# Feed-forward column pairs as seven block products of input sums, and a window V load divided at row 2

## The chip, the cores and the metric

The kernel runs on one core of one Trainium2 chip. The metric is the device time of one execution in microseconds. The kernel before took 1517.5 us in the median of three runs (1512.81 to 1521.79).

## What is computed

One step of a decoder layer for 520 tokens: a prompt of 512 and 8 sampled tokens. The core of the reference, cut:

```python
x = x + 0.5 * swiglu(rms_norm(x, ffn1_norm), ffn1_w_in, ffn1_w_out)
mixed, state = token_mixers(rms_norm(x, mix_norm), ...)
x = x + mixed
x = x + 0.5 * swiglu(rms_norm(x, ffn2_norm), ffn2_w_in, ffn2_w_out)
return rms_norm(x, final_norm), state

def swiglu(h, w_in, w_out):          # w_in 1024 x 5632, w_out 2816 x 1024
    a, b = split(h @ w_in, 2)
    return (silu(a) * b) @ w_out
```

The mixers are a causal convolution group and an attention group with three branches (compressed, selected and sliding-window keys and values); the sampled tokens read paged caches and a window of 512 earlier tokens of each sequence. Everything is float32.

## The kernel before

**Layout.** Activations lie transposed: 128 partitions hold features, 520 columns hold tokens, so X is 8 tiles (k = 0 to 7) of 128 x 520. `HALF` names the two token halves of 260 columns. A product in float32 is made of three matmuls in a reduced format (`mm3`): weight high x input high, weight high x input low, weight low x input high, where high is a rounded copy (made on ACT by `acp`) and low is the rest (made on DVE or POOL by a subtraction).

**Stages.** The program runs in this order: compression of the cached keys and values (`compress`), the first feed-forward layer, the input projection, convolution and attention under a planner (`Threads`, which keeps a modelled clock for each engine and always steps the earliest thread), the output projection (`t_wout`), the second feed-forward layer, the final norm (`tail`). In the feed-forward layers nothing is planned: the order is the order of the code.

**A feed-forward layer** (`ffn`, line 763) works in three groups of 8, 7 and 7 column pairs (`GROUPS`). A column pair is 128 gate columns and 128 value columns of `w_in`. For each pair and each token half it makes the gate product and the value product over k = 0 to 7, each in a PSUM bank of its own: 2 x 2 x 8 x 3 = 96 matmuls of 128x260. Then `gate` (silu on ACT), `value` (the product with the gate on DVE, its high part on ACT) and `low` (its low part on DVE) follow, one step later each. In the second layer the norm is not in the inputs: `gate` and `value` first multiply the PSUM result by `r`. After a group come four output blocks (`d2`) of `w_out` columns with four accumulations each, added to X on DVE.

**Weights** (`Units`, line 711). A block of weights is 1 MB, loaded on SP's queue into one of two buffers `wraw` (tag raw). It is cut into units of 128x512: for each unit ACT makes the high part and DVE the low part in one of 4 tiles `wb` of two units each, so at most 8 units are ahead of TensorE. `step` issues the pending low parts, at most one new unit, the matmuls, and then what the plan holds for this step. When the last low part of a block has been issued, `w_dma` issues the load of the block after the next.

**Around the layers.** The first layer's inputs `xh`, `xl` are normalised while `compress` runs (`xp_scale`, `xp_low`). `bg` holds small work on the compressed keys (`kc_root`, `kc_norm`) of which one piece goes behind each block of the first layer; `bg_out` holds transposes (`kc_trans`, `conv_state`) for the last group's output blocks. The compressed V, `vcs`, stays in buffer B1 from the compression until attention reads it.

**The window** (`win_load`, line 1682). For a sampled sequence b, the window buffer holds 512 positions as 128 rows of 4 x 128 values; one position, the first quarter of row 0, is that of the new token and comes from `ksm`. Keys are loaded as 128 rows and V as three DMAs: rows 1 to 127 (line 1688), the rest of row 0 (line 1689), the new token (line 1690). Two sequences' keys go to a buffer of their own and the others, with all V, rotate through four buffers `kwr`, so that V of sequences 4 to 7 is loaded when TensorE has read V of sequences 0 to 3. All of them are issued on SP's queue, in order.

Names in the profile: pb is a PSUM bank; xh and xl the layer's inputs; wb the weight units; gh and gl the gated products; late the window buffers; sg the gathered selected blocks; misc holds ksm; line 120 is the helper that issues every engine instruction.

Of the kernel before, what the change touches and what calls it, by code (L numbers as in the profile page):

```python
# [19 lines left out]
NB = 8  # L20
# [13 lines left out]
PF = 2  # L34
XP = 0
# [171 lines left out]
def tile_step(ctx: ExitStack, tc: tile.TileContext, I, O, off):  # L207
# [318 lines left out]
    vcs = new("B1", [2, NB, 128], F32, "vcs")  # L526
    hl_i = [0]
# [12 lines left out]
    def compress():  # L540
# [69 lines left out]
        soft.append(lambda: cmp_second(*pend, 5))  # L610
# [7 lines left out]
    def xp_scale(k):  # L618

        if k == 0:  # L620
            X1["h"] = rows("A2", 8, F32R, "xh")
            X1["l"] = Rows([new("B0", [4, T], F32R, "xl"), None])
        if k == 4:
            X1["l"].tiles[1] = new("A1", [4, T], F32R, "xl")
        t = X1["t"] = tmp([T])
        tt(t, X[:, k], R["r0"], ALU.mult)
        acp(X1["h"][:, k], t, scale=g1(k))
# [4 lines left out]
    def u_start():  # L632
        U1.append(Units(0))
# [77 lines left out]
    class Units:  # L711


        def __init__(self, c0):
            self.c, self.list, self.pp, self.hl, self.low = c0, [], 0, {}, []
            self.pf, self.n = PF if c0 else 8, {}
            for j0, n in GROUPS:
                for j in range(n + 4):
                    self.n[c0] = 2048 if j < n else n * 256
                    self.list += [(c0, q) for q in range(4)]  # L720
                    c0 += 1
            self.left = [2] * (len(self.list) // 2)

        def more(self):
# [4 lines left out]
            c, q = self.list[i_]  # L729
            if i_ % 2 == 0:  # L730
                self.cur = new(("WH", "WL")[i_ // 2 % 2], [2, 2, 512], F32R, "wb", 2)
            m = min(512, self.n[c] - q * 512)
            x = wraw[c][:, q * 512:q * 512 + m]
            h, l = self.cur[:, i_ % 2, 0, :m], self.cur[:, i_ % 2, 1, :m]
# [6 lines left out]
            if q == 3:  # L741
                self.low.append(c)
            self.pp += 1
            return True

# [13 lines left out]
        def used(self, c):  # L759
            for q in range(4):  # L760
                self.left[self.hl.pop((c, q))[2]] -= 1

    def ffn(U, xh, xl, normed, bg, next_prep, g_tiles, tail=None, out=(), last=None):
# [3 lines left out]
        r = None if normed else new("r", [T])  # L767
# [4 lines left out]
        def step(work):  # L772
            nonlocal q_
            U.lows()
            U.more()
# [7 lines left out]
        if r is not None:  # L783
            put(0, lambda: norm_root(r, R["acc"], D, (6, 7)), partial(recip, 0), partial(recip, 1))
            put(1, partial(recip, 2), partial(recip, 3))
        while soft:
            put(0, soft.pop(0))
        for gi, (j0, n) in enumerate(GROUPS):
            gh, gl = g_tiles(n)
            for j in range(n):  # L790
                for h in range(2):
                    o_ = (2 * j + h + (0 if n == 8 else 2)) % 4 * 2
                    pa, pb = [ps.tile([128, 512], F32, name="pb", tag="b%d" % (o_ + s_))[:, :TH] for s_ in range(2)]
                    t = tmp([2, TH])

                    def prods(o, s_, h=h):
                        first = gi == 0 and j == 0
                        for k in range(8):
                            w_ = U.parts(c, k, s_ * 128)
                            mm(o, w_[0], xh[:, k, HALF[h]], k == 0, False)  # L800
                            if not first:
                                mm(o, w_[0], xl[:, k, HALF[h]], False, False)
                            mm(o, w_[1], xh[:, k, HALF[h]], False, k == 7 and not first)
                        for k in range(8) if first else ():
                            mm(o, U.parts(c, k, s_ * 128)[0], xl[:, k, HALF[h]], False, k == 7)

                    def gate(t=t, pa=pa, h=h):
                        if r is not None:
                            tt(t[:, 0], pa, r[:, HALF[h]], ALU.mult)
                            pa = t[:, 0]  # L810
                        ACT.activation(t[:, 0], pa, AF.Silu)

                    def value(t=t, pb=pb, h=h, g=gh[:, j, HALF[h]]):
                        if r is not None:
                            tt(t[:, 1], pb, r[:, HALF[h]], ALU.mult)
# [1372 lines left out]
```

## Time and profile before

| | before |
|---|---|
| median of 3 runs, us | 1517.5 (1512.81 to 1521.79) |
| the profiled execution, us | 1514.12 |
| its span, first to last instruction, us | 1512.3 |
| mean granted TensorE clock | 0.957 |
| TensorE busy | 1378.9 us, 91% |
| DVE busy | 835.3 us, 55% |
| ACT busy | 597.8 us, 40% |
| POOL busy | 321.8 us, 21% |
| HBM traffic | 108 GB/s over the span |

The profile is one execution. A line of its groups names the source line, engine, operation, output <- inputs, shape and count, then busy time and the mean length of one in ns, then the engine's idle time just before and what ended it. Matmuls overlap, so the length of one (283 ns) is not what one costs; cost is taken from counts per time. A busy share is an average over stages with different limits, so each stage is read by itself.

### The profile page before, as it was taken

Reading aid. Unit: us, or ns where it says so; the run is one execution under the profiler, and the core shown is the slowest. Engines: PE = TensorE matmul, PEld = TensorE weight load, DVE = VectorE, ACT = ScalarE, POOL = GpSimd, SP = SyncE. Lnnn points to the kernel's source line nnn. Section 1 sums busy time; section 2 is a strip of 40 time slices with the busy share of each in tenths; the row PEclk is TensorE's granted clock in tenths of the full one; section 3 lists DMA queues with packets and bytes.
Section 4 is the critical chain, followed back from the end, with each engine's and each line's share of the span. In section 5 each row is a group of like instructions: output and inputs, shape, how many; then the busy total and the mean of one; then the engine's idle time right before and its main releaser. Section 6 shows DMA issues by size and latency. Waiting matters only on the chain.

```text
span 1512.3 us, 25566 instructions
## 1 busy us (share of the span) xinstructions
PE 1378.9 (91%) x10375; PEld 1271.8 (84%) x10375; DVE 835.3 (55%) x1670; ACT 597.8 (40%) x1280; POOL 321.8 (21%) x286
## 2 busy tenths in 40 slices
PE   3999898999999999997888899926899999999997
PEld 2778676999999999997686776716899999999997
DVE  3777789334334433679796556624684534444444
ACT  2445455333232233456566635404343322322333
POOL 4556755000000000145464022113220000000000
PEclk8999999999999999999899889958799999999999
DMA  5846353222332333242129035405133233233321
GB/s 170 250 144 195 112 163 116 57 85 84 110 87 74 109 86 111 83 141 79 36 86 222 28 83 161 147 29 136 61 96 96 84 101 96 81 99 87 95 102 57
DMA packets 168824, 160.25 MB, mean 106 GB/s; under 512 B 9013, under 2 KB 150933, under 8 KB 168507
## 3 DMA queue, kind: packets, MB, share of 16 engines
q1 hardware_dynamic: 153859, 109.33, 24.3%
q0 software_dynamic: 14848, 49.29, 10.9%
q8 instruction: 81, 1.33, 0.4%
q14 instruction: 36, 0.29, 0.1%
HBM read 152.65 MB, written 10.60 MB: 108 GB/s over the span
## 4 chain that ended last, share of the span: by engine, by line
PE 39%; DVE 7%; ACT 3%; SPq 3%; DMA 2%; issue 1%; POOL 0%; DVEq 0%; POOLq 0%; ACTq 0%
PE pb L120 39%; SPq L1689 2%; DVE cv L120 1%; DVE tmp L120 1%; DVE wl L120 1%; DVE misc L120 1%; ACT pz L120 1%; DMA late<-misc 1%; ACT tmp L120 0%; ACT L120 0%; ACT wh L120 0%; DMA sg<-in_cache_v_sel,idxs 0%; DVE su L120 0%; SPq L322 0%; DVE usm_v L120 0%
## 5 line engine op out<-in xcount | busy, mean ns | idle before, releaser
L120 PE MATMUL pb<-xh,wb 128*128 128x260 f32 x2816 | 501.5, 283 | 0.8 <-ACT wb L120 0.5
L120 PEld LDWEIGHTS pb<-xh,wb 128*128 128x128 f32 x2816 | 430.2, 188 | 1.4 <-ACT wb L120 0.7
L120 PE MATMUL pb<-xl,wb 128*128 128x260 f32 x1408 | 387.9, 282 | 0.0
L120 PEld LDWEIGHTS pb<-xl,wb 128*128 128x128 f32 x1408 | 261.0, 188 | 0.0
L120 PE MATMUL pb<-gh,wb 128*128 128x260 f32 x1408 | 256.6, 283 | 0.0
L120 ACT ACTIVATE wb<-wraw 128x512 fp32r<-128x512 f32 (+1 forms) x272 | 161.1, 610 | 175.7 <-PE pb L120 158.8
L120 PEld LDWEIGHTS pb<-gh,wb 128*128 128x128 f32 x1408 | 218.0, 188 | 0.0
L120 PE MATMUL pb<-gl,wb 128*128 128x260 f32 x704 | 198.7, 282 | 0.0
L120 DVE TENSOR_TENSOR wb<-wraw,wb 128x512 fp32r<-128x512 f32 (+1 forms) x262 | 174.7, 667 | 2.1
L120 PEld LDWEIGHTS pb<-gl,wb 128*128 128x128 f32 x704 | 132.5, 188 | 0.0
L120 PE MATMUL pb<-hl,w1hl 128*128 128x512 f32 x384 | 99.3, 408 | 14.2 <-DVE hl L120 13.8
L120 DVE TENSOR_TENSOR tmp<-pb,r 128x260 f32<-128x260 f32 x104 | 43.6, 426 | 123.2 <-PE pb L120 123.2
L120 DVE TENSOR_TENSOR hl<-tmp,hl 128x512 fp32r<-128x512 f32 x128 | 92.7, 724 | 32.1 <-ACT hl L120 18.5
L120 DVE SCALAR_TENSOR_TENSOR X<-pb,X 128x260 f32<-128x260 f32 x96 | 41.0, 428 | 123.8 <-PE pb L120 123.8
L120 DVE TENSOR_TENSOR tmp<-pb,tmp 128x260 f32<-128x260 f32 x44 | 18.9, 429 | 161.8 <-PE pb L120 157.1
L120 ACT ACTIVATE gh<-tmp 128x260 fp32r<-128x260 f32 x88 | 37.2, 423 | 171.9 <-DVE tmp L120 170.2
L120 ACT ACTIVATE hl<-tmp 128x512 fp32r<-128x512 f32 x128 | 79.1, 630 | 62.0 <-DVE tmp L120 50.3
L120 PEld LDWEIGHTS pb<-hl,w1hl 128*128 128x128 f32 x384 | 70.5, 190 | 38.5 <-DVE hl L120 23.3
L120 DVE STREAM_TRANSPOSE tmp<-craw 128x512 f32<-128x512 f32 x128 | 89.6, 701 | 23.5 <-issue 10.3
L120 PE MATMUL pb<-hl,w1h 128*128 128x512 f32 x256 | 85.6, 412 | 4.8 <-DVE hl L120 2.9
L120 POOL TENSOR_TENSOR wl<-wraw,wh 128x512 fp32r<-128x512 f32 (+1 forms) x23 | 34.9, 1519 | 215.8 <-ACT wh L120 204.8
L120 POOL DMA_INDIRECT craw<-in_cache_k_cmp,idxc x64 | 63.9, 998 | 57.8 <-DVE tmp L120 33.3
(307 smaller groups left out, 2319.5 us busy)
## 6 DMA issues: line engine op xcount, KB each, us to landing
wraw<-in_ffn_w_in SPq DMA_DIRECT2D x88, 512.0 KB
wraw<-in_ffn_w_out SPq DMA_DIRECT2D x16, 896.0 KB
wraw<-in_ffn_w_out SPq DMA_DIRECT2D x8, 1024.0 KB
wraw<-in_w_in SPq DMA_DIRECT2D x8, 512.0 KB
wraw<-in_w_in SPq DMA_DIRECT2D x4, 1024.0 KB
wraw<-in_w_out SPq DMA_DIRECT2D x4, 1024.0 KB
xs<-X SPq DMA_DIRECT2D x1, 2080.0 KB
X<-xs SPq DMA_DIRECT2D x8, 260.0 KB
```

What stands on the lines that cost most here:

```text
L120: r = fn(*a, **k)
L1689: SP.dma_start(t_[0:1, 128:512], src[0:1, 128:512])
```

## The change

It has two parts, and the buffers and order that they need.

**Seven products.** Each layer gets a string of kinds per group, one letter for each pair: P plain, S seven products. The change is announced as 16 of 22 pairs; `KINDS1` and `KINDS2` hold 14 letters S each. For an S pair the inputs are four blocks (two token halves by two halves of k) and the weights four blocks (two halves of k by gate and value). Seven products of 4 k-tiles each, of blocks or of sums of blocks (Winograd's form), replace eight. Four of the weight operands are differences made on DVE in the raw buffer or in a temporary; the four input sums (`Sums`) are made once per layer, from normalised inputs, on POOL, with their high and low parts on ACT and DVE. The results are put together by additions on DVE as they leave PSUM. Two of the banks are read by DVE after their first product and written again by TensorE later. In the second layer the blocks themselves are also normalised once (`blocks`, `b21`), so pairs after the first four need no multiplication by `r`.

**Pace and order.** P pairs now go through all four banks for every quarter of k, so that a unit is used up in one step of 24 matmuls (12 in an S step). `pace` issues units at a rate that depends on the kind (0.9 a step in S, 1.5 in P, 1.25 in output blocks), `need` makes one that isn't there. The first output block of each group goes by quarters of k too.

**Buffers.** B1, D0, D1, D2 and A1 hold the sums. So the compressed V is written to DRAM after the compression (`vsp`) and read back in the last group's output blocks; `kc_trans` and `conv_state` come 6 places later there.

**The window.** V is loaded as rows 2 to 127, then columns 128 to 511 of rows 0 and 1, then the first quarter of row 1, then the new token.

The core of the diff:

```diff
+KINDS1 = "PPPSSPSS", "SSPSSPS", "SSPSSPS"
+KINDS2 = "PPPPSSSS", "SSPSSPS", "SSPSSPS"
+RATE = {"S": .9, "P": 1.5, "O": 1.25}
...
+        def last():
+            cmp_second(*pend, 5)
+            SP.dma_start(vsp, vcs)
+        soft.append(last)
...
+        def source(self, c, q):
+            if self.kind[c] != "S":
+                m = min(512, self.n[c] - q * 512)
+                return wraw[c][:, q * 512:q * 512 + m]
+            v = wraw[c][:, :2048].rearrange("p (k h e) -> p k h e", k=8, h=2)
+            b11, b12, b21, b22 = v[:, 0:4, 0], v[:, 0:4, 1], v[:, 4:8, 0], v[:, 4:8, 1]
+            if q == 1:
+                tt(b11, b12, b11, ALU.subtract)
+                self.t2 = tmp([4, 128])
+                tt(self.t2, b22, b11, ALU.subtract)
+            if q == 2:
+                tt(b12, b22, b12, ALU.subtract)
+            if q == 5:
+                tt(b21, b21, self.t2, ALU.subtract)
+            return (b11, self.t2 if q else None, b12, b11, b21, b21, b22)[q]
...
+        def pace(self, rate):
+            self.credit = min(self.credit + rate, 2.5)
+            self.lows()
+            while self.credit >= 1 and self.more():
+                self.credit -= 1
+                if self.credit >= 1:
+                    self.lows()
...
+                for o_, p_, q_, op in ((st[0][:, 0], a[:, HALF[1]], b[:, HALF[1]], ALU.add),
+                                       (st[0][:, 1], None, a[:, HALF[0]], ALU.subtract),
+                                       (st[1][:, 0], a[:, HALF[0]], a[:, HALF[1]], ALU.subtract),
+                                       (st[1][:, 1], b[:, HALF[0]], None, ALU.subtract)):
+                    POOL.tensor_tensor(o_, st[0][:, 0] if p_ is None else p_, st[0][:, 1] if q_ is None else q_, op=op)
...
-        def step(work):
+        def step(work, kind):
             nonlocal q_
-            U.lows()
-            U.more()
+            U.pace(RATE[kind])
             work()
...
+        for kk in range(4):
+            for i_ in range(3):
+                put((1 if normed else 3) + 3 * kk + i_ - (kk > 2 and normed),
+                    lambda kk=kk, i_=i_: parts_.setdefault(kk, SX.prep(kk, r, gname))[i_]())
...
+        def seven(c, j, bk, G):
+            p_, q2, r_, s_ = bk
...
+            s0 = q_
+            put(s0 + 1, lambda: acp(u[:, 0], p_))
+            put(s0 + 2, lambda: tt(u[:, 0], q2, u[:, 0], ALU.add))
+            put(s0 + 3, lambda: tt(u[:, 1], r_, u[:, 0], ALU.add))
+            put(s0 + 4, lambda: tt(tb[:, 1], s_, u[:, 1], ALU.add))
+            put(s0 + 5, lambda: ACT.activation(ta[:, 0], p_, AF.Silu))
+            put(s0 + 6, lambda: tt(tb[:, 0], r_, u[:, 0], ALU.add),
+                lambda: ACT.activation(tb[:, 0], tb[:, 0], AF.Silu))
+            put(s0 + 7, lambda: tt(ta[:, 1], s_, u[:, 0], ALU.add), lambda: tt(ta[:, 1], ta[:, 1], ta[:, 0], ALU.mult),
+                lambda: acp(ga[0], ta[:, 1]), lambda: tt(tb[:, 1], tb[:, 1], tb[:, 0], ALU.mult),
+                lambda: acp(gb[0], tb[:, 1]))
+            put(s0 + 8, lambda: tt(ga[1], ta[:, 1], f(ga[0]), ALU.subtract),
+                lambda: tt(gb[1], tb[:, 1], f(gb[0]), ALU.subtract))
+            for q, (o, x_, first, end) in enumerate((
+                    (p_, a(0, 0), True, False), (q2, s(2), True, True), (r_, s(3), True, False),
+                    (s_, s(1), True, False), (p_, a(0, 1), False, True), (r_, a(1, 1), False, True),
+                    (s_, s(4), False, True))):
...
+        vcs = new("B1", [2, NB, 128], F32, "vcs")
+        SP.dma_start(vcs, vsp)
...
-    bg_out = [bg_loads, lambda: None]
+    bg_out = [bg_loads] + [lambda: None] * 7
...
-        SP.dma_start(t_[1:128], src[1:128])
-        SP.dma_start(t_[0:1, 128:512], src[0:1, 128:512])
+        SP.dma_start(t_[2:128], src[2:128])
+        SP.dma_start(t_[0:2, 128:512], src[0:2, 128:512])
+        SP.dma_start(t_[1:2, 0:128], src[1:2, 0:128])
         SP.dma_start(t_[0:1, 0:128], ksm[b:b + 1, 1, 1])
```

More of the change, by code (lines that the diff above doesn't have):

```diff
@@ L744, in more, with need @@
             return True
+        def pace(self, rate):
[5 more added lines that the diff above has]
+                    self.lows()
+        def need(self, c, q):
+            while (c, q) not in self.hl:
+                self.lows()
+                assert self.more()
+                self.credit -= 1
         def lows(self):
@@ new lines, in evac, with gate, value, low @@
+        def evac(o, j, g, un):
+            for h in range(2):
+                t = tmp([2, TH])
+                def gate(t=t, pa=o[0, h], h=h):
+                    if un:
+                        tt(t[:, 0], pa, r[:, HALF[h]], ALU.mult)
+                        pa = t[:, 0]
+                    ACT.activation(t[:, 0], pa, AF.Silu)
+                def value(t=t, pb=o[1, h], h=h, g=g[h][0]):
+                    if un:
+                        tt(t[:, 1], pb, r[:, HALF[h]], ALU.mult)
+                        pb = t[:, 1]
+                    tt(t[:, 1], pb, t[:, 0], ALU.mult)
+                    acp(g, t[:, 1])
+                def low(t=t, g=g[h][0], l=g[h][1]):
+                    tt(l, t[:, 1], f(g), ALU.subtract)
+                put(q_ + h, gate, value)
+                put(q_ + h + 1, low)
@@ L788, in ffn @@
         for gi, (j0, n) in enumerate(GROUPS):
-            gh, gl = g_tiles(n)
+            G = g_tiles(n)
             for j in range(n):
[L791 to L815, printed above, removed]
-                            pb = t[:, 1]
-                        tt(t[:, 1], pb, t[:, 0], ALU.mult)
-                        acp(g, t[:, 1])
-                    def low(t=t, g=gh[:, j, HALF[h]], l=gl[:, j, HALF[h]]):
-                        tt(l, t[:, 1], f(g), ALU.subtract)
-                    put(q_ + 1, gate)
-                    put(q_ + 2, value)
-                    put(q_ + 3, low)
-                    step(lambda: prods(pa, 0))
-                    step(lambda: prods(pb, 1))
-                U.used(c)
@@ new lines, in ffn @@
+                o_ = (j + (0 if n == 8 else 1)) % 2 * 4
+                bk = [ps.tile([128, 512], F32, name="pb", tag="b%d" % (o_ + s_))[:, :TH] for s_ in range(4)]
+                if U.kind[c] == "S":
+                    if SX.b21 is None and SX.b:
+                        SX.b21 = make(True)
+                        for kk in range(4):
+                            put(q_ + 6 * kk + 1, partial(SX.rest, kk, r, gname))
+                    seven(c, j, bk, G)
+                else:
+                    plain(c, j, bk, G)
@@ L1980, in tile_step @@
     c_ffn2 = c_mix + 13
-    U2 = Units(c_ffn2)
+    U2 = Units(c_ffn2, KINDS2)
     def t_units():
```

192 lines of the change are left out of this document (155 added, 37 removed).

## The prediction

> **What bounds the kernel now.** I read the page first, for where TensorE is busy.
>
> ```profile
> span 1512.3 us, 25566 instructions
> PE   3999898999999999997888899926899999999997
> PEclk8999999999999999999899889958799999999999
> ```
>
> Each digit is a fortieth of the span, 37.8 us. Two long runs of 9 are the feed-forward layers (about 264 to 650 and 1117 to 1503 us); the hole "26" near 1000 us is the end of the attention stage. The stage table gives the rates (columns: PE busy with its count, weight loads, DVE, ACT, POOL, granted clock, DMA share, GB/s).
>
> ```profile
> 300.00:600.00 300.00, 300.00 (x2515) 300.00 (x2515) 116.38 (x245) 93.02 (x190) 6.17 (x4) 1.00 0.31 91
> 1150.00:1450.00 300.00, 300.00 (x2502) 300.00 (x2502) 136.56 (x287) 89.36 (x181) 0.00 (x0) 1.00 0.32 93
> 984.00:1025.00 41.00, 7.18 (x56) 5.81 (x56) 6.79 (x8) 1.19 (x2) 5.01 (x4) 0.53 0.07 25
> 1025.00:1119.00 94.00, 79.94 (x707) 75.25 (x707) 64.29 (x115) 41.10 (x81) 33.83 (x27) 0.86 0.36 99
> ```
>
> In the feed-forward layers TensorE never pauses and a matmul costs 300 / 2515 = 0.119 us; DVE is busy 39% and 46%, ACT 31%. So a matmul taken away there is worth 0.119 us as long as DVE keeps up. From 984 to 1025 every engine is idle while DMA runs at a share of 0.07, about one of 16 engines, at 25 GB/s. TensorE's waits say what for, first in the first layer (255 to 660 us), then between the layers (660 to 1030 us); columns are total, times, longest.
>
> ```profile
> PE pb L120 <- DVE hl L120: 2.0, 2, 1.2
> ```
>
> ```profile
> PE pb L120 <- DMA late<-misc: 34.4, 4, 9.8
> ```
>
> The timeline of the hole shows SP's queue and TensorE:
>
> ```profile
> 976.00 4.75 SPq L1971 DMA_DIRECT2D X<-xs  x8
> 981.30 0.26 SPq L1688 DMA_DIRECT2D late<-in_state_v_win  x1
> 981.60 3.62 SPq L1689 DMA_DIRECT2D late<-in_state_v_win  x1
> 985.27 0.52 SPq L1690 DMA_DIRECT2D late<-misc  x1
> 985.89 0.37 SPq L1688 DMA_DIRECT2D late<-in_state_v_win  x1
> 986.31 7.46 SPq L1689 DMA_DIRECT2D late<-in_state_v_win  x1
> 1014.66 2.04 SPq L1690 DMA_DIRECT2D late<-misc  x1
> 1025.58 1.87 PE L120 MATMUL pb<-late,slate 128*4 128x64 f32 x16 [8.42 <-DMA late<-misc]
> ```
>
> A 127-row load of V (254 KB) moves at 25 GB/s, so 10 us each; four in a row are the hole. TensorE goes on at 1025.6 + 1.9 = 1027.5.
>
> **The products.** The two strings of kinds hold 4 + 5 + 5 = 14 letters S per layer, not 16, so 28 pairs in all. A pair was 96 matmuls of 260 columns and is 7 x 4 x 3 = 84 as S. Removed: 28 x 12 = 336, which the program order confirms (6336 before, 6000 after). 336 x 0.119 = **40.0 us** off the path, if nothing replaces it. The same matmul form stays, so no other price enters.
>
> **What DVE must do for it.** Its prices in the first layer, by shape (busy, mean ns), and three neighbours in the timeline (start, duration):
>
> ```profile
> L120 DVE TENSOR_TENSOR wb<-wraw,wb 128x512 fp32r<-128x512 f32 x103 | 70.3, 684 | 1.8
> L120 DVE TENSOR_TENSOR tmp<-pb,tmp 128x260 f32<-128x260 f32 x38 | 16.3, 429 | 134.3 <-PE pb L120 134.3
> L120 ACT ACTIVATE wb<-wraw 128x512 fp32r<-128x512 f32 x102 | 62.0, 624 | 76.5 <-PE pb L120 72.6 <-ACT hsq L120 3.9
> L120 ACT ACTIVATE gh<-tmp 128x260 fp32r<-128x260 f32 x38 | 16.1, 423 | 71.5 <-DVE tmp L120 71.5
> ```
>
> ```profile
> 299.86 0.43 DVE L120 TENSOR_TENSOR tmp<-pb,tmp 128x260 f32<-128x260 f32 x1 [3.42 <-PE pb L120]
> 300.20 0.68 DVE L120 TENSOR_TENSOR wb<-wraw,wb 128x512 fp32r<-128x512 f32 x1
> 300.80 0.42 DVE L120 TENSOR_TENSOR gl<-tmp,gh 128x260 fp32r<-128x260 f32 x1
> ```
>
> Neighbours overlap: 0.34 us from start to start after a 260-wide one, 0.60 after a 512-wide one. This is DVE in the second layer before, one pair and the start of the next, pb the products, r the norm, wb the weights' low parts:
>
> ```order
> L120 TENSOR_TENSOR tmp_12110<-pb_12108,r_10554 128x260
> L120 TENSOR_TENSOR wb_12112<-wraw_11928,wb_12112 128x512
> L120 TENSOR_TENSOR tmp_12110<-pb_12109,r_10554 128x260
> L120 TENSOR_TENSOR tmp_12110<-tmp_12110 128x260
> L120 TENSOR_TENSOR wb_12177<-wraw_12050,wb_12177 128x512
> L120 TENSOR_TENSOR gl_12044<-tmp_12110,gh_12043 128x260
> L120 TENSOR_TENSOR tmp_12172<-pb_12170,r_10554 128x260
> ```
>
> and after, in a pair of seven products of the second layer, where the rows that write wraw or read it into tmp form the weights' differences:
>
> ```order
> L123 TENSOR_TENSOR tmp_12346<-pb_12343,tmp_12346 128x260
> L123 TENSOR_TENSOR wb_12368<-wraw_12169,wb_12368 128x512
> L123 TENSOR_TENSOR wraw_12169<-wraw_12169 128x4x128
> L123 TENSOR_TENSOR tmp_12404<-wraw_12169 128x512
> L123 TENSOR_TENSOR tmp_12346<-pb_12344,tmp_12346 128x260
> L123 TENSOR_TENSOR wb_12402<-tmp_12404,wb_12402 128x512
> L123 TENSOR_TENSOR wraw_12169<-wraw_12169 128x4x128
> L123 TENSOR_TENSOR tmp_12348<-pb_12345,tmp_12346 128x260
> ```
>
> The norm's products are gone; differences stand ahead of the sums that read pb_12344 and pb_12345, banks that TensorE writes again two products later. A pair S costs DVE 7 lows, 4 differences and 9 operations of 260: 11 x 0.60 + 9 x 0.34 = 9.7 us, 11.4 at full durations. TensorE takes 84 x 0.119 = 10.0. A pair P costs DVE 4 x 0.60 + 4 x 0.34 = 3.8 against 96 x 0.119 = 11.4. Two S and a P: 23.2 to 27.3 us on DVE against 31.4. Walking the rows: after the bank's first product DVE has two products, 2 x 12 x 0.119 = 2.9 us, and ahead of its sum stand at most one low and two differences, 1.8 to 2.1. So steady groups cost TensorE about nothing; I put 2 us for the norm work of the compressed keys that shares DVE in the first layer. ACT needs 7 x 0.62 + 5 x 0.42 = 6.4 of 10.0.
>
> **The starts of the layers** are tighter, since there the sums of inputs are made, on POOL and DVE. Here is what POOL does to DVE's operations on SBUF, and POOL's price and the norm's:
>
> ```profile
> 1098.96 1.31 POOL L120 TENSOR_TENSOR wl<-wraw,wh 128x512 fp32r<-128x512 f32 x1 [0.79 <-ACT wh L120]
> 1099.22 1.34 DVE L120 TENSOR_TENSOR X<-tmp,X 128x260 f32<-128x260 f32 x1
> 1102.20 0.43 DVE L120 TENSOR_TENSOR X<-tmp,X 128x260 f32<-128x260 f32 x1
> L120 POOL TENSOR_TENSOR otok<-otok,tmp 128x256 f32<-128x256 f32 x6 | 5.7, 944 | 59.4 <-DVE otok L120 45.5 <-PE pb L120 13.8
> 1122.31 0.97 DVE L120 RECIPROCAL r<-r 128x130 f32<-128x130 f32 x1 [2.64 <-ACT r L120]
> ```
>
> The same DVE row takes 0.43 alone and 1.34 beside POOL. The change adds 16 POOL operations of 260 per layer, 16 x 0.94 = 15 us, beside which DVE can lose 0 to 15. [...]
>
> First layer, steps before the first S: some 30 operations of 512 or 520, 8 of 260, 2 reductions: 21 to 25 us against 3 x 11.4 = 34.3; with POOL up to 40. Stall 0 to 5, I take 3. Second layer, from the reciprocals to the first S's first sum: 44 of 512 or 520, 46 of 260, 4 reciprocals: 45.6 to 53.7 us against 4 x 11.4 = 45.7, and 0 to 15 for POOL. Then four S in a row, with four small preparations of 2 x 0.43 among them: 42 to 49 us against 40.0. DVE ends 2 to 32 us late over both, 2.9 of it free. I take 8 (the sums are ordered first, and the weights stand up to 8 units, 11 us, ahead), ends 0 to 23. All stalls: 3 + 8 + 2 = **13 us**, 2 to 30.
>
> **The window loads.** SP before (late: the window buffers):
>
> ```order
> L2063 DMA out_s_v_win<-in_state_v_win 8x4x16352
> L1510 DMA sg<-misc 1x16x4 x4
> L1971 DMA X<-xs 128x520 x8
> L1688 DMA late<-in_state_v_win 127x512
> L1689 DMA late<-in_state_v_win 1x384
> L1690 DMA late<-misc 1x16x8
> ```
>
> and after:
>
> ```order
> L2253 DMA out_s_v_win<-in_state_v_win 8x4x16352
> L1699 DMA sg<-misc 1x16x4 x4
> L2161 DMA X<-xs 128x520 x8
> L1877 DMA late<-in_state_v_win 126x512
> L1878 DMA late<-in_state_v_win 2x384
> L1879 DMA late<-in_state_v_win 1x128
> L1880 DMA late<-misc 1x16x8
> ```
>
> One issue more per load, and 126 rows. The nearest rows: loads of 128 and of 120 rows are not slow. Key loads of 128 rows (L1686) are issued in 0.56 each; the two 120-row loads of the conv state (480 KB, issued at 600.0 beside a weight load) are over by 606:
>
> ```profile
> 815.82 2.25 SPq L1686 DMA_DIRECT2D late<-in_state_k_win  x4
> 600.00:606.00 6.00, 6.00 (x52) 6.00 (x52) 1.37 (x4) 2.49 (x5) 0.00 (x0) 1.00 0.76 235
> 606.00:611.00 5.00, 5.00 (x44) 5.00 (x43) 1.85 (x4) 1.96 (x5) 0.00 (x0) 1.00 0.00 0
> ```
>
> On one engine those 480 KB would have run to 619. So I take 126 rows as fast: four loads x four issues x 0.5 = 8 us from 981.3, about 2 to land (a small DMA), 1.9 of matmuls: TensorE goes on at 993 instead of 1027.5, **34 us** earlier. Ends: 25 (2 us per issue, the longest L1690) and 38. [...] What is late next: the selected V gathers, which wait for TensorE and move up as a block, since DVE, ACT and POOL idle in the hole. The clock, 0.53 in the hole and 0.86 after it, falls less: 3 us (0 to 8).
>
> **The rest.** The second layer's first pair no longer needs the last X rows at once: 0.45 + 0.34 us of waits go, 1 us:
>
> ```profile
> 1119.00 0.39 PE L120 MATMUL pb<-xh,wb 128*128 128x260 f32 x1 [0.45 <-ACT wb L120]
> 1119.72 0.63 PE L120 MATMUL pb<-xh,wb 128*128 128x260 f32 x3 [0.34 <-DVE wb L120]
> ```
>
> Compressed V goes to DRAM and back, 1 MB each, on SP ahead of weight loads. A weight block of 1 MB moves in 5 us:
>
> ```profile
> 379.00:384.00 5.00, 5.00 (x45) 5.00 (x44) 2.06 (x4) 1.94 (x4) 0.00 (x0) 1.00 0.77 213
> 384.00:390.00 6.00, 6.00 (x53) 6.00 (x52) 2.42 (x5) 0.00 (x0) 0.22 (x1) 1.00 0.00 0
> ```
>
> Weights have 6.4 us even after a P that is split at 0.9 units a product, so 5 us more delay one block by 4, which the units ahead cover; without that cover, 4 us each. The spill waits on SP for ACT's last copy of V, the return for TensorE's last product of sums; weight loads are queued behind both. DVE's first difference now waits for weights where ACT did; behind it stand the sums that free the banks, but with weights there in time it costs nothing. Eight copies of the conv state move to the first layer's last block, nearer to a start that DVE bounds: 8 x 0.43 = 3.4 at most, 2 taken.
>
> **Sum**, on the profiled execution's 1514.1 (its span and 1.8 outside): -40.0 - 34 - 3 - 1 + 13 + 2 = -63, so 1451. It lies 3.4 under the median 1517.5, so I forecast **1454**. Ends: -40 - 38 - 8 - 1 + 2 + 0 = -85, or 1432; -40 - 25 + 30 + 4 = -31, or 1486.
>
> **Rivals.**
> 1. The 126-row load stays on one engine: no 34, no 3. 1454 + 37 = 1491. Against it: 120 rows were fast. 0.04.
> 2. DVE becomes the bound in every S, slower than before. Each low waits out its ACT copy (0.62) because difference, copy and low follow one another: 11.4 + 7 x 0.62 = 15.7 us a pair, 5.7 over, 28 x 5.7 = 160 us. 1454 - 13 + 2 + 160 = 1603. It is slower than before from (40 + 34 + 4 - 2) / 28 = 2.7 us over, 12.7 us a pair. For it: the order above has such a chain. Against: only the second difference's low follows closely, the others come a product later. 0.04.
> 3. POOL blocks DVE wholly at both starts: 5 + 23 + 2 = 30 us of stalls instead of 13: 1471. 0.14.
> 4. No stall at all, units ahead cover the starts: 1454 - 13 = 1441. 0.13.
>
> **Chances.** The forecast, within 10 us, 0.65. The range 1432 to 1486 holds all but the first two rivals and the tails. About 0.5%, 8 us, is what a measurement here can tell from no change. Faster by over 0.5%: 0.94 (all but the second rival and a failure of both parts); within: 0.02; slower: 0.04.
>
> **What would show it.** Right: 6000 matmuls of 260 columns; TensorE unbroken through the groups of S and P, pauses only in the first 60 us of each layer, on DVE; V loads with issues under 1 us; no row of late<-misc among TensorE's long waits. Wrong: TensorE waiting on DVE tmp in every S, DMA share 0.07 for tens of us, or POOL rows with DVE rows over 1 us beside them all along.

## The result and the profile after

The changed kernel takes 1471.3 us in the median (1469.5 to 1471.5 in three runs; a fourth, at 1850 us with a clock of 0.65, is left out) against 1515.2 for the kernel before. The ratio is 0.970, interval 0.965 to 0.976: faster, by 44 us where 63 were forecast. The profiled execution took 1471.5 us, its span 1469.6.

The page of the changed kernel, first its busy times, then TensorE and its clock in 40 slices:

```profile
span 1469.6 us, 25507 instructions
PE 1339.1 (91%) x10039; PEld 1230.6 (84%) x10039; DVE 1017.1 (69%) x1986; ACT 662.3 (45%) x1424; POOL 347.9 (24%) x318
PE   3999889989999999999788889987997899999997
PEclk8999999999999999999989999997999999999999
```

The hole "26" is gone, and TensorE has 336 products fewer; its busy time is 39.8 us shorter. There are two new dents, an 8 in the ninth slice and "78" after the 9s of the second layer's beginning: 294 to 331 us and 1102 to 1176 us.

The stages (columns as in the prediction) show that the loss lies near the starts of the layers:

```profile
300.00:325.00 25.00, 19.01 (x141) 18.17 (x141) 20.33 (x36) 12.20 (x27) 7.08 (x8) 0.94 0.16 43
375.00:625.00 250.00, 250.00 (x2086) 249.82 (x2085) 169.87 (x345) 101.69 (x210) 6.11 (x4) 1.00 0.35 103
1125.00:1150.00 25.00, 13.76 (x83) 13.15 (x84) 20.05 (x41) 11.66 (x26) 2.00 (x2) 0.80 0.15 43
1175.00:1450.00 275.00, 274.99 (x2292) 274.61 (x2291) 173.81 (x344) 104.53 (x217) 0.00 (x0) 1.00 0.32 95
```

In the second and fourth rows a product costs 0.120 us and TensorE never pauses, with DVE 68% and 63% busy. In the first and third it gets through 141 and 83 products where a stretch of 25 us holds 209.

Where a layer begins and ends is read from TensorE's timeline (start, duration), here the first row of the first layer and its last, then those of the second (its last row begins with the first of seven products, the seventh at 1459.5):

```profile
271.49 0.28 PE L123 MATMUL pb<-xh,wb 128*128 128x260 f32 x1
645.58 0.29 PE L123 MATMUL pb<-gh,wb 128*128 128x260 f32 x1
1073.13 0.28 PE L123 MATMUL pb<-xh,wb 128*128 128x260 f32 x1
1458.74 0.99 PE L123 MATMUL pb<-g,wb 128*128 128x260 f32 x7
```

The same reading of both traces divides the 42.7 us between the two spans:

| stretch | before | after | difference |
|---|---|---|---|
| start to the first layer's first product | 264.2 | 271.5 | +7.3 |
| first layer | 381.7 | 374.1 | -7.6 |
| to the reload of X (X<-xs) | 330.0 | 322.8 | -7.2 |
| reload to the last product with the window's V | 51.1 | 18.4 | -32.8 |
| to the second layer's first product | 89.8 | 86.4 | -3.4 |
| second layer | 386.0 | 386.3 | +0.3 |
| end | 9.4 | 10.2 | +0.8 |

A layer without stalls would be 14 x 12 x 0.119 = 20.0 us shorter than before. So 12.4 us were lost in the first layer and 20.3 in the second, which has no gain left.

The window loads, on SP and then on TensorE, and TensorE's wait for them between the layers (total, times, longest):

```profile
973.68 0.35 SPq L1877 DMA_DIRECT2D late<-in_state_v_win  x1
974.08 0.26 SPq L1878 DMA_DIRECT2D late<-in_state_v_win  x1
974.38 0.25 SPq L1879 DMA_DIRECT2D late<-in_state_v_win  x1
975.10 0.52 SPq L1880 DMA_DIRECT2D late<-misc  x1
980.96 3.56 PE L123 MATMUL pb<-late,slate 128*4 128x64 f32 x32 [4.04 <-DMA late<-misc]
```

```profile
PE pb L123 <- DMA late<-misc: 4.0, 1, 4.0
```

Each of the four issues takes under 0.6 us and TensorE waits 4.0 us where it waited 34.4.

At the second layer's start (1070 to 1180 us) TensorE waits for this:

```profile
PE pb L123 <- DVE tmp L123: 8.1, 6, 3.6
PE pb L123 <- DVE xb L123: 5.7, 1, 5.7
PE pb L123 <- ACT tmp L123: 1.8, 1, 1.8
PE pb L123 <- ACT xb L123: 0.3, 1, 0.3
```

The longest, 5.7 us, stands inside the first S pair's first product, whose last k-tile waits for the low part of the normed block xb. Here is what stands ahead of it, ACT's rows (the first makes xb's high part), DVE's, then TensorE's:

```profile
1124.73 1.02 ACT L123 ACTIVATE xb<-tmp 128x260 fp32r<-128x260 f32 x3
1127.58 0.40 ACT L123 ACTIVATE tmp<-tmp 128x260 f32<-128x260 f32 x1
1128.47 0.42 ACT L123 ACTIVATE g<-tmp 128x260 fp32r<-128x260 f32 x1 [0.49 <-DVE tmp L123]
1128.80 0.61 ACT L123 ACTIVATE wb<-wraw 128x512 fp32r<-128x512 f32 x1
1128.01 0.43 DVE L123 TENSOR_TENSOR tmp<-tmp 128x260 f32<-128x260 f32 x1 [0.80 <-ACT tmp L123]
1129.44 0.69 DVE L123 TENSOR_TENSOR wb<-wraw,wb 128x512 fp32r<-128x512 f32 x1 [1.00 <-ACT wb L123]
1130.17 0.69 DVE L123 TENSOR_TENSOR wraw<-wraw,tmp 128x512 f32<-128x512 f32 x1
1130.78 1.10 DVE L123 TENSOR_TENSOR xb<-tmp,xb 128x260 fp32r<-128x260 f32 x3
1131.26 0.80 PE L123 MATMUL pb<-xb,wb 128*128 128x260 f32 x2 [5.68 <-DVE xb L123]
```

The low of xb needs only the first of these rows, which ends at 1125.75. It starts at 1130.78, since it stands behind the others in DVE's queue. In these 5.0 us DVE works 3.2 and waits for ACT 1.8: 0.80 for a silu, 1.00 for the copy of a weight unit that had just been queued. From the reciprocals to this product the stage's busy times and then DVE's waits are:

```profile
1077.00:1131.26 54.26, 45.12 (x372) 44.33 (x370) 40.02 (x73) 24.53 (x52) 13.39 (x16) 0.97 0.29 78
```

```profile
DVE wb L123 <- ACT wb L123: 7.8, 7, 3.2
DVE tmp L123 <- ACT tmp L123: 6.2, 6, 4.6
DVE r L123 <- ACT r L123: 1.3, 1, 1.3
```

DVE has 40.0 us of work in 54.3 us; it waits for ACT for 15.3 us, 1.1 of them ahead of this window. The longest of these waits, 4.6 us, is for a silu that stood in ACT's queue behind six copies, a wait of 0.5 us for POOL's sums and 1.28 us of loading a table; the 3.2 us are for a copy behind ACT's waits for POOL (1.4 and 0.8).

### The profile page after: what moved, and what is told of

It reads as the page before. It is cut to its first block, busy times and chain, and to the rows that moved or that the text cites. A ratio compares the mean times of both kernels' runs of the same rounds, so it can differ in the third digit from the quotient of the medians.

```text
span 1469.6 us, 25507 instructions
## 1 busy us (share of the span) xinstructions
PE 1339.1 (91%) x10039; PEld 1230.6 (84%) x10039; DVE 1017.1 (69%) x1986; ACT 662.3 (45%) x1424; POOL 347.9 (24%) x318
## 3 DMA queue, kind: packets, MB, share of 16 engines
q8 instruction: 79, 1.29, 0.4%
## 4 chain that ended last, share of the span: by engine, by line
PE 34%; DVE 12%; ACT 5%; issue 2%; DMA 1%; POOL 1%; SPq 0%; POOLq 0%; DVEq 0%; ACTq 0%
PE pb L123 34%; DVE tmp L123 3%; DVE cv L123 2%; DVE misc L123 1%; DVE wl L123 1%; DVE wb L123 1%; ACT pz L123 1%; ACT tmp L123 1%; POOL tmp L123 1%; ACT wb L123 1%; ACT L123 1%; ACT wh L123 0%; DVE wraw L123 0%; DMA sg<-in_cache_v_sel,idxs 0%; DMA late<-misc 0%
## 5 line engine op out<-in xcount | busy, mean ns | idle before, releaser
L123 ACT ACTIVATE wb<-wraw 128x512 fp32r<-128x512 f32 x328 | 190.4, 612 | 255.1 <-PE pb L123 141.4
L123 PE MATMUL pb<-xh,wb 128*128 128x260 f32 x1104 | 205.7, 284 | 7.3 <-DVE tmp L123 6.3
L123 PE MATMUL pb<-xl,wb 128*128 128x260 f32 x776 | 200.9, 284 | 0.0
L123 PEld LDWEIGHTS pb<-xh,wb 128*128 128x128 f32 x1104 | 173.2, 189 | 8.4 <-DVE tmp L123 6.9
L123 PEld LDWEIGHTS pb<-xl,wb 128*128 128x128 f32 x776 | 141.4, 190 | 0.3 <-DVE tmp L123 0.2
L123 PE MATMUL pb<-sh,wb 128*128 128x260 f32 x672 | 132.3, 286 | 2.7 <-ACT sh L123 2.3
L123 PE MATMUL pb<-g,wb 128*128 128x260 f32 x1056 | 128.7, 283 | 0.0
L123 PE MATMUL pb<-gh,wb 128*128 128x260 f32 x704 | 128.6, 283 | 0.0
L123 PE MATMUL pb<-sl,wb 128*128 128x260 f32 x448 | 127.7, 285 | 0.5 <-DVE sl L123 0.5
L123 PEld LDWEIGHTS pb<-g,wb 128*128 128x128 f32 x1056 | 127.2, 188 | 0.0
L123 PE MATMUL pb<-hl,w1hl 128*128 128x512 f32 x384 | 102.1, 413 | 15.1 <-DVE hl L123 13.3
L123 DVE STREAM_TRANSPOSE tmp<-craw 128x512 f32<-128x512 f32 x128 | 89.5, 700 | 22.2 <-DMA craw<-in_cache_k_cmp,idxc 15.2
```

The lines of the kernel that those rows point to most:

```text
L123: r = fn(*a, **k)
```

## The experiments

Layer lengths are read in each trace as above; a length holds to 0.1 us where the code is the same (374.1 and 374.0, 386.3 and 386.4). "Over" is the length less that of before minus 1.43 us for each S pair. The whole time is less sharp: the first layer began between 253.6 and 271.5 us and the stretch between the layers took 420.7 to 437.7 us in runs that have the new window load and the new feed-forward code. Small effects are therefore judged by the layers, whose length holds TensorE's waits and also a slower clock behind them (last section): a product at half clock starts 0.22 us after the one before, at full clock 0.12.

| run | S pairs | median us | ratio to before, interval | first layer, over | second layer, over |
|---|---|---|---|---|---|
| changed kernel | 14, 14 | 1471.3 | 0.970 (0.965 to 0.976) | 374.1, 12.4 | 386.3, 20.3 |
| window loads alone | 0, 0 | 1461.9 | 0.978 (0.975 to 0.981) | 381.7, 0 | 386.0, 0 |
| pairs alone | 14, 14 | 1488.0 | 0.995 (0.992 to 0.997) | 374.0, 12.3 | 386.4, 20.4 |
| sums on DVE | 14, 14 | 1447.3 | 0.969 (0.966 to 0.972) | 373.4, 11.7 | 384.6, 18.6 |
| all plain | 0, 0 | 1458.9 | 0.978 (0.975 to 0.982) | 383.5, 1.8 | 383.5, -2.5 |
| pace 1.2 | 14, 14 | 1450.3 | 0.967 (0.960 to 0.975) | 373.5, 11.8 | 381.1, 15.1 |
| copies first | 14, 14 | 1441.1 | 0.961 (0.955 to 0.967) | 370.2, 8.5 | 383.9, 17.9 |
| late preparations later | 14, 14 | 1451.3 | 0.967 (0.961 to 0.973) | 374.1, 12.4 | 388.2, 22.2 |
| sevens later | 12, 12 | 1448.6 | 0.964 (0.957 to 0.970) | 368.2, 3.7 | 387.0, 18.2 |
| three changes | 13, 14 | 1460.9 | 0.968 (0.963 to 0.973) | 367.4, 4.3 | 380.6, 14.6 |
| sums closer | 14, 14 | 1459.4 | 0.969 (0.962 to 0.976) | 372.6, 10.9 | 384.8, 18.8 |
| sevens without sums | 14, 14 | 1444.2 | 0.959 (0.953 to 0.964) | 366.6, 4.9 | 370.7, 4.7 |
| four changes | 13, 14 | 1443.1 | 0.965 (0.961 to 0.970) | 367.4, 4.3 | 378.0, 12.0 |

The kernel before took 1497.0, 1502.7, 1507.3 and 1495.0 us on the chips of the four groups of runs (first four, next four, next three, last), so ratios are compared, not medians.

**Which part gave what.** The window loads alone, put into the kernel before:

```diff
-        SP.dma_start(t_[1:128], src[1:128])
-        SP.dma_start(t_[0:1, 128:512], src[0:1, 128:512])
+        SP.dma_start(t_[2:128], src[2:128])
+        SP.dma_start(t_[0:2, 128:512], src[0:2, 128:512])
+        SP.dma_start(t_[1:2, 0:128], src[1:2, 0:128])
```

> The kernel before, with the V window load divided at row 2 and nothing else. The traces of before and after differ by 43.4 us between the last product of the first feed-forward layer and the first of the second, and by nothing in the sum of all else. Theory (the window loads gave the whole gain, the pairs of seven products nothing net): 1515 - 43 = 1472 us, ratio 0.971. Rival (the loads gave what was forecast for them, 34 of the hole and 3 of the clock, and the pairs a net gain of 6 or more): 1478 us, ratio 0.9755. First product of the first layer at 264 us if its shift of 7.3 us belongs to the pairs, at 271 us if it is not the change's.

Measured: -33 us (28 to 38). That is the rival's ratio, not the theory's. From the reload of X to the last product with V it takes 16.4 us instead of 51.1, the forecast's 34; TensorE's waits between the layers hold

```profile
PE pb L120 <- DMA late<-misc: 2.0, 1, 2.0
```

The first layer begins at 257.1 here, at neither of the two places expected.

The opposite, the old load in the changed kernel (the diff above backwards):

> The changed kernel with the old V window load of 127 and 1 rows: the pairs of seven products alone. Theory (stalls at the two starts eat the 40 us of products): 1515 us, between 1508 and 1517, with the first layer about 374 us long and the second about 386. Rival (the forecast's terms, -40 + 13 + 2, the rest of the difference lying in the loads): 1490 us.

Measured: ratio 0.995, -8 us (4 to 12), with the layers as the theory has them; they explain it, 7.7 and -0.4. TensorE's wait is the old one:

```profile
PE pb L123 <- DMA late<-misc: 34.6, 4, 10.0
```

The theory was wrong in making it nothing, since it had charged the late first layer to the change. With the same code for everything ahead of the first layer it begins at 256.1 here and at 271.5 in the changed kernel's profile, so that is the run's. So are the 7.2 us saved ahead of the reload, in part at least: before and the run of the loads alone had a stretch of 24 us at half clock there, 212 to 238 us after the first layer; this run and the changed kernel had 3.4 us. What sets it is open.

**Is it the pairs, or the order and pace around them?** All pairs plain, no sums made (the diff without the buffer of g's upper half):

```diff
-KINDS1 = "PPPSSPSS", "SSPSSPS", "SSPSSPS"
-KINDS2 = "PPPPSSSS", "SSPSSPS", "SSPSSPS"
+KINDS1 = "PPPPPPPP", "PPPPPPP", "PPPPPPP"
+KINDS2 = "PPPPPPPP", "PPPPPPP", "PPPPPPP"
...
-        put(1 if normed else 2, sums)
...
```

> The changed kernel with every pair plain (P): no pair of seven products, no sums, 6336 products of 260 columns; the new order inside a pair, the new pace of conversions, the copy of compressed V to DRAM and back and the new window loads stay. (The upper half of g in the second layer stands in another buffer.) Theory (the stalls come from the pairs of seven and their sums): both layers run without a stall, 382 and 386 us as before, so the time is that of the window loads alone, 1472 us, between 1468 and 1476. Rival (the new order and pace cost by themselves): 1480 us or more, with TensorE's waits on DVE at the starts although no sums are made.

Measured: as the loads alone (0.978 both). The second layer's first 92 us, with DVE busy 48 us, run without a pause:

```profile
1064.00:1156.00 92.00, 92.00 (x769) 91.88 (x768) 48.33 (x101) 34.63 (x68) 0.00 (x0) 1.00 0.36 104
```

The new order, pace and the copy of V through DRAM cost nothing in sum: the first layer is 1.8 us longer than before, the second 2.5 shorter.

**Is it the sums, or the pairs' own additions?** The S pairs kept, the sums and the normed blocks left out (so that the products are not the layer's; the core of the diff):

```diff
-                return lambda kk: SX.get(i_ - 1, kk)
+                return lambda kk: inp(kk, (i_ - 1) % 2, True)
...
```

> The changed kernel without the sums: the pairs of seven products keep their order, their 84 products, the differences of their weights and their additions after the products, but read the input and its low part where they read a sum or a normed block, and nothing is made at the start of a layer. (The upper half of g in the second layer stands in another buffer.) Theory M (what stalls is the sums' work at the starts, in whatever form): first layer 361.7 and at most 1, second 366 and at most 1.5. Rival S (the first pairs of seven stall by their own additions and differences): first layer 366 or more, second 372 or more, with TensorE's waits on DVE tmp of 2.8 and 3.8 us still there.

Measured: 4.9 and 4.7 us over. The first layer, 366.6 us, just meets S's bound; the second, 370.7, lies between the two. The sums and blocks account for 7.5 of the 12.4 us and 15.6 of the 20.3. The rest comes with the pairs; in the second layer TensorE still waits, mostly once, in the first S pair:

```profile
PE pb L123 <- DVE tmp L123: 3.6, 4, 2.7
```

**Is it POOL?** The 32 additions of the sums on DVE:

```diff
-                    POOL.tensor_tensor(o_, st[0][:, 0] if p_ is None else p_, ...
+                    DVE.tensor_tensor(o_, st[0][:, 0] if p_ is None else p_, ...
```

> The changed kernel with the 32 additions of the input sums (two layers) moved from POOL to DVE, which pays 0.34 us for one where POOL took 0.84 to 0.99. Theory L (the sums come late because a block of four on POOL takes 3.2 to 4.0 us and ACT's and DVE's queues stand behind it): the stalls shrink, 1471 - 8 = 1463 us, between 1459 and 1466. Rival D (DVE has no room at the starts; whatever is added there is added to the stall): 16 x 0.34 = 5.4 us more a layer, 1471 + 5 to 11 = 1476 to 1482 us.

Measured: 0.7 and 1.7 us less. Both failed. The run changes two things at once, POOL's part and DVE's work, and they may cancel: from the reciprocals to the first sum of the first S pair DVE is busy 53.7 us instead of 50.2 and idle 10.9 instead of 15.8. It shows that the two together are worth little, not that each is.

**Is it DVE waiting in its queue, or the amount of its work?** First both of a step's copies ahead of its lows (where no S pair follows, whose differences overwrite what a low reads):

```diff
-                if self.credit >= 1:
+                if self.credit >= 1 and self.pp < len(self.list) and self.kind[self.list[self.pp][0]] == "S":
                     self.lows()
...
             while (c, q) not in self.hl:
...
+            if any(not isinstance(x_, int) and x_[0] is self.hl[c, q][1] for x_ in self.low):
+                self.lows()
```

> The changed kernel, but where two units of a plain pair or of the output projection are converted in one step, both of ACT's copies are queued before the first low on DVE, which so no longer stands waiting for the copy just issued (0.5 to 1.0 us each time; DVE waits 9.6 us in 11 such places from 1073 to 1165 us). Theory W (DVE falls behind at the starts because in its queue it waits for ACT): up to 10 us less, second layer 386.4 to 379, between 376 and 382, first 374.0 to 371. Theory M (what counts is the amount of DVE's work): no more than 2 us less in either.

Measured: 3.8 and 2.5 us less: what W says in the first layer, little over M's bound in the second. TensorE's waits there fell by 3.9 us, from 15.9 to 12.0, but about 18 more products ran at half clock, which took back 1.8. DVE's waits over 92 us fell where they were meant to (9.6 to 5.0), but not the others:

```profile
DVE tmp L123 <- ACT tmp L123: 6.4, 7, 4.6
DVE wb L123 <- ACT wb L123: 5.0, 8, 1.0
```

Then fewer conversions ahead:

```diff
-RATE = {"S": .9, "P": 1.5, "O": 1.25}
+RATE = {"S": .9, "P": 1.2, "O": 1.25}
...
```

The rest of the diff is the second part of the one above, which queues a low that the step needs.

> The changed kernel with 1.2 units of weights converted a step in plain pairs where it converts 1.5. In the changed kernel the first layer lasts 374.0 us from its first product of 260 columns to its last, the second 386.4, each the same in two profiles; without a stall they would be 361.7 and 366. Theory M (DVE has more to do before the first pairs of seven than it can): in the four plain pairs of the second layer 16 x 0.3 = 5 units fewer, 3 us of DVE, so 383 us there and 372 in the first. Rival K (the units ahead are what carries the pairs of seven, which convert 0.9 a product): with fewer ahead these wait for weights, second layer 390 us or more, first 376 or more.

Measured: 5.3 us less in the second layer, 0.5 in the first. That is M's direction, with more than the 3 us of work taken away; no product waited for weights, so K falls. But the amount of work is not what changed: to the first sum of the first S pair DVE is busy 49.8 us instead of 50.2, and idle 10.5 instead of 15.8.

**Does another place in the queue help?** The sums 2 steps apart:

```diff
-                put((1 if normed else 3) + 3 * kk + i_ - (kk > 2 and normed),
+                put((1 if normed else 3) + 2 * kk + i_,
```

> The changed kernel with the four preparations of the sums 2 steps apart instead of 3 in both layers, so that the last low of the blocks is queued on DVE at step 11 instead of 14 of the second layer, whose first pair of seven begins at step 16, and at step 9 instead of 11 in the first layer (step 12). Theory T (the first pair of seven waits, 5.9 us in the second layer and 3.3 in the first, because its sums are queued late): these waits fall below 2.5 and 1, second layer 386.4 to 382, first 374.0 to 371. Theory M (DVE has more to do than time for): the wait moves to the plain pairs, whose banks DVE then frees later, and both layers stay within 1.5 us.

Measured: 1.4 and 1.6 us less, M's 1.5 within 0.1. The wait for xb is gone, and as M has it another has come, 5.7 us in a plain pair whose bank DVE had not read:

```profile
PE pb L123 <- DVE tmp L123: 9.6, 5, 5.7
PE pb L123 <- ACT tmp L123: 3.9, 1, 3.9
```

The late preparations moved behind:

```diff
-                            put(q_ + 6 * kk + 1, partial(SX.rest, kk, r, gname))
+                            put(q_ + 5 * kk + 8, partial(SX.rest, kk, r, gname))
```

> The changed kernel with the four late preparations of the second layer (the blocks of the second half's first rows, each a multiplication and a low on DVE and a copy on ACT) at products 8, 13, 18 and 23 behind the first pair of seven instead of 1, 7, 13 and 19. Theory R (the wait of 1.9 us at 1137 for ACT, and part of the 3.8 at 1141 for DVE, come from them): second layer 386.4 to 383, first layer unchanged at 374.0. Rival (they only shift the same wait): 386 in the second layer.

Measured: 388.2, 1.8 us more in the second layer, so both missed. The waits that R names did shrink, from 1.8 to 0.2 us and from 3.6 to 2.7, but waits of 1.1 and 1.8 us came behind them. In sum TensorE waits 15.4 us instead of 15.9, and the layer is longer because about 27 more products run at half clock. Moving these preparations only moves the wait.

**Does more time ahead help?**

```diff
-KINDS1 = "PPPSSPSS", "SSPSSPS", "SSPSSPS"
-KINDS2 = "PPPPSSSS", "SSPSSPS", "SSPSSPS"
+KINDS1 = "PPPPPPSS", "SSPSSPS", "SSPSSPS"
+KINDS2 = "PPPPSSPP", "SSPSSPS", "SSPSSPS"
...
-                put((1 if normed else 3) + 3 * kk + i_ - (kk > 2 and normed),
+                put(1 + 6 * kk + i_ if normed else 3 + 3 * kk + i_,
...
-                            put(q_ + 6 * kk + 1, partial(SX.rest, kk, r, gname))
+                            put(q_ + 3 * kk + 1, partial(SX.rest, kk, r, gname))
```

> The changed kernel with fewer and later pairs of seven in the first group of each layer: first layer PPPPPPSS in place of PPPSSPSS, its sums spread over 22 steps instead of 12; second layer PPPPSSPP in place of PPPPSSSS, its four late preparations 3 products apart. 24 more products in each layer, 2.9 us. Theory M (the starts lack time on DVE): first layer 381.7 - 12 x 1.43 = 364.6 and 0 to 2 of stalls, 366 us instead of 374.0; second layer: the wait of 9 us before its first pair of seven stays, those behind it (8 us with the lower clock) go, 386.4 + 2.9 - 8 = 381 us. Rival S (each first pair of seven after plain ones costs its 4 to 8 us wherever it stands): first layer 370 us or more, second layer 386 or more.

Measured: in the first layer, where the sevens really begin later, 3.7 us over instead of 12.4, so two S pairs fewer are 5.9 us faster; 368.2 us lies between M's 366 and S's 370. In the second layer M missed: 387.0, past S's bound. There the first seven is still the fifth pair and the wait stays; plain pairs behind it gain 2.1 us of stall for 2.9 us of products. The sevens cannot begin later there as the buffers stand: from the fifth pair on, g takes the place of xh, and a plain pair would need the block that `rest` makes.

**Together.** A first attempt (copies first, 1.2 units, PPPPPSSS with sums 4 steps apart in the first layer, sums 2 steps apart in the second):

```diff
-KINDS1 = "PPPSSPSS", "SSPSSPS", "SSPSSPS"
+KINDS1 = "PPPPPSSS", "SSPSSPS", "SSPSSPS"
...
-RATE = {"S": .9, "P": 1.5, "O": 1.25}
+RATE = {"S": .9, "P": 1.2, "O": 1.25}
...
-                put((1 if normed else 3) + 3 * kk + i_ - (kk > 2 and normed),
+                put(1 + 4 * kk + i_ if normed else 3 + 2 * kk + i_,
...
```

> A version meant to be faster: the changed kernel with both copies ahead of the lows (which took 3.8 and 2.5 us off the layers), 1.2 units a step in plain pairs (0.5 and 5.3 us off), the first layer's first group PPPPPSSS (13 pairs of seven in the layer instead of 14) with its sums 4 steps apart instead of 3, and the second layer's sums 2 steps apart instead of 3. Theory M (work on DVE ahead of the first pair of seven): first layer 381.7 - 13 x 1.43 + 3 = 366 us; second 386.4 - 2.5 - 5.3, less 3 for the earlier sums = 375.6, between 374 and 379. Both together 18 us less than the changed kernel's 760.4, ratio to the kernel before 0.958. Rival S (each first pair of seven after plain ones costs 4 to 8 us wherever it stands): second layer 380 or more, first 369 or more.

Measured: the first layer (367.4) near M's number, the second (380.6) 5 us over it and just past S's bound. And a second, with the second layer's sums 3 steps apart again and the additions on DVE:

```diff
-                put(1 + 4 * kk + i_ if normed else 3 + 2 * kk + i_,
+                put(1 + 4 * kk + i_ if normed else 3 + 3 * kk + i_,
...
-                    POOL.tensor_tensor(o_, st[0][:, 0] if p_ is None else p_, ...
+                    DVE.tensor_tensor(o_, st[0][:, 0] if p_ is None else p_, ...
```

> The changed kernel with what shortened a layer by itself: both copies ahead of the lows (3.8 and 2.5 us), 1.2 units a step in plain pairs (0.5 and 5.3), the additions of the sums on DVE (0.7 and 1.7), and in the first layer PPPPPSSS with the sums 4 steps apart; the second layer's sums stay 3 steps apart. If these add: second layer 386.4 - 2.5 - 5.3 - 1.7 = 377 us, between 375 and 380; first 367, between 365 and 369; together 16 us less than in the changed kernel, ratio to the kernel before 0.960. If they take away the same wait and don't add: second layer 381 or more, and no faster than the changed kernel by more than 10 us.

Measured: 367.4 and 378.0, so the gains nearly add: the layers are 15.0 us shorter than in the changed kernel. It beats the kernel before by 3.5% (3.0 to 3.9). Against the changed kernel the ratios, 0.965 and 0.970, have intervals that overlap, so only the layers show the gain. Here are the second layer's first 92 us in the changed kernel, then in this one with TensorE's longest wait:

```profile
1073.00:1165.00 92.00, 76.98 (x600) 75.42 (x599) 71.59 (x139) 42.28 (x90) 13.39 (x16) 0.94 0.25 69
```

```profile
1048.70:1140.70 92.00, 83.31 (x653) 81.83 (x652) 81.22 (x168) 46.04 (x96) 0.00 (x0) 0.94 0.29 81
```

```profile
PE pb L123 <- ACT tmp L123: 5.4, 1, 5.4
```

DVE is now 88% busy, against 78%, and the longest wait is for ACT. What the last 12 us of that layer would need is open.

## Why the prediction was right in its sign and 17 us off

- **Products, -40.** Right: 336 fewer, and in the stretches at full rate one costs 0.120 us. That TensorE's busy time fell by 39.8 us is in part luck, since it also counts products at half clock: with all 336 still there it was 1378.9, 1370.3 and 1362.7 us (before, loads alone, all plain).
- **Window loads, -34.** Right: 34.8 us by the loads alone, 32.8 in the changed kernel. The first rival falls: from 982 to 983 us the third load of 126 rows moved at a DMA share of 0.75 and 236 GB/s, where those of 127 had 0.07 and 25. Why, no run shows. The 2 us to land were the author's estimate; in the changed kernel 5.3 us passed from the end of the first load's last issue (975.62) to TensorE's first product behind its wait (980.96). 3 us for the clock behind the hole: 3.2 to 3.4.
- **Steady groups cost TensorE nothing.** Right: full rate from 375 to 625 and from 1175 to 1450 us. The second rival, DVE the bound in every S pair, falls. So do the fears for the copy of V through DRAM and for the weights.
- **Second layer's first pair no longer waits, -1; the conv state, +2.** Small; the run of plain pairs has the second layer 2.5 us shorter and the first 1.8 longer than before, which fits both, but they weren't tried one by one.
- **All stalls, 13.** This is the step that failed: 32.7 us, 12.4 in the first layer (3 + 2 forecast) and 20.3 in the second (8 forecast), just past the upper end of 30. That end was too low by the prediction's own numbers: DVE up to 32 us late with 2.9 free leaves 29 for the second layer, where it wrote 23 without a working. The lengths of the layers hold the -1 and the +2 as well, so 32.7 stands against 14, and the sum becomes 1451 + 18.7 = 1469.7, against a profiled 1471.5; its other misses (first layer 7.3 us late, 7.2 us gained ahead of the reload) cancel. The fourth rival, no stall at all, falls.

The step set DVE's busy time against the time there was, from the reciprocals to the first sum of the first S pair. The amount of work was right: 45.6 to 53.7 us forecast, 50.2 found. The time was 4.0 us shorter than the 45.7 written, since the reciprocals come that long after the layer's first product. And DVE was not busy all along: the first row is this stretch in the changed kernel, the second in the last run above.

```profile
1077.12:1143.11 65.99, 53.00 (x420) 51.79 (x418) 50.23 (x95) 28.93 (x61) 13.39 (x16) 0.95 0.29 80
```

```profile
1052.69:1109.85 57.16, 50.78 (x416) 50.36 (x415) 52.07 (x109) 28.68 (x60) 0.00 (x0) 0.97 0.34 93
```

DVE stood idle for 15.8 us, nearly always for a result of ACT, while work that TensorE needed stood behind; in the last run it did more work and was idle 5.1, and the layer's loss fell from 20.3 to 12.0. What the step left out is that DVE takes its work in order (the low of xb could start at 1125.75 and did at 1130.78) and shares each small job with ACT: normed block, copy, low; product, silu, product. The second rival had such a wait of a low for its copy, but in the steady groups, where it cost nothing. An estimate from these numbers: without a pause the 50.2 us of work, against 41.7 for the plain pairs and 2.9 for two products, would be some 6 us late, so the 8 forecast would have covered the amount alone. Shown of this: without the waits for fresh copies the layers are 3.8 and 2.5 us shorter; with fewer conversions in the way 0.5 and 5.3; with more plain pairs ahead and two S pairs fewer, the first layer's stall falls to 3.7. Moving the sums' work within the same stretch mostly moves the wait. Not shown: a single cause for the whole 20.3 us, nor what each of DVE's waits is worth, since in one run its idle time fell by 2.4 us for 2.5 of the layer, in another by 4.9, with 3.5 us more work, for 1.7.

The third rival named 1471, the number measured, and its cause did not hold. It had POOL block DVE for 15 us a layer; in both layers together 11 DVE rows beside POOL's 32 additions are stretched, by 5.2 us in all. Here are POOL's four additions and DVE's rows beside them:

```profile
1123.23 3.77 POOL L123 TENSOR_TENSOR tmp<-tmp 128x260 f32<-128x260 f32 x4 [9.19 <-DVE tmp L123]
1122.97 0.76 DVE L123 TENSOR_TENSOR tmp<-pb,r 128x260 f32<-128x260 f32 x2
1124.29 1.24 DVE L123 TENSOR_TENSOR wb<-wraw,wb 128x512 fp32r<-128x512 f32 x1
```

The low with both inputs in SBUF takes 1.24 instead of 0.69 us, and the low of g behind it (1125.45) 0.96 instead of 0.42; the products that read a PSUM bank keep their 0.42 each. All 11 stretched rows have two SBUF inputs, but such a row can also keep its time: a product at 1123.94 takes its 0.43, a low at 309.52 its 0.69. The rival had counted every DVE row as blocked, for all of POOL's time.

## What to carry to other kernels

When an engine is given more small jobs, its busy share does not tell whether it keeps up (over the second layer's first 92 us DVE was 78% busy where the layer lost 20.3 us, and 88% where it lost 12.0): where two engines hand each job back and forth in order, count the waits in the queue, above all ahead of the first instruction that a third engine waits for. Where there is room, start such work so that several pairs lie between it and its first use, and queue a copy some instructions ahead of what reads it. And before a new method is credited, put each part of a change in alone: here the plain part, three lines that load the window, gave 33 of 44 us.

## What the runs showed of the hardware that was not expected

**Some waits cost more than their length.** In the traces of before and after the clock has two levels, 1.00 and 0.50. During the wait of 5.7 us it fell to 0.5 and stayed there for 6.8 us (the first row), then it was full again (the second); behind the waits of 1.8 and 3.6 us it was 0.5 for another 3.3 us (the third):

```profile
1127.80:1134.60 6.80, 3.35 (x15) 3.35 (x16) 5.55 (x12) 2.79 (x6) 0.00 (x0) 0.50 0.00 0
1134.60:1137.30 2.70, 2.70 (x25) 2.70 (x23) 2.55 (x8) 0.87 (x3) 0.00 (x0) 1.00 0.50 141
1144.90:1148.20 3.30, 3.30 (x17) 3.30 (x17) 2.37 (x6) 0.70 (x2) 0.00 (x0) 0.50 0.02 5
```

15 products in 3.35 us of running are 0.22 us each against 0.12 in the steady groups, so the first stretch cost 1.5 us on top of its wait, the second 1.3. Over the whole second layer some 39 more products than in the kernel before start 0.22 us after the one ahead of them. That adds about 3.9 us to TensorE's 15.9 us of waits, 19.8 of the 20.3. The first halving, at 1127.8, came 2.2 us after TensorE's last product ended (1125.6); a wait of 2.4 us that ended at 1111.4 left the clock at 1.00. What decides when the clock falls, no run shows.

**POOL can be the one that takes longer.** In the run with copies first, DVE had five operations on SBUF without a pause, two of them in the second row, and POOL's first addition took 3.00 us where four took 3.77 above:

```profile
1069.87 3.00 POOL L123 TENSOR_TENSOR tmp<-tmp 128x260 f32<-128x260 f32 x1 [9.42 <-DVE tmp L123]
1069.96 1.28 DVE L123 TENSOR_TENSOR wb<-wraw,wb 128x512 fp32r<-128x512 f32 x2
```

DVE keeps its pace, 1.28 us for two overlapping lows (1.29 with POOL idle, at 1133.36 in the changed kernel).
